# Seven block products in place of eight in two feed-forward chunks of each layer, with weight sums formed by accumulating transfers

## The chip, the core and the metric

The kernel runs on one core of a Trainium2 chip. A core has TensorE (PE, matrix products; its weight loads are shown apart as PEld), VectorE (DVE), ScalarE (ACT), GpSimd (POOL) and SyncE (SP). SP and POOL also start transfers, which all run on the core's 16 DMA engines. The metric is the device time of one execution in microseconds (us). Less is better.

## The reference, cut to what matters

Two layers over 256 positions of width 1024 in float32. Each layer has a mixing half and a feed-forward half; the change is in the second:

```
h2 = rms_norm(x, ln2_g[l])
x = x + (jax.nn.silu(h2 @ w_ff_gate[l]) * (h2 @ w_ff_up[l])) @ w_ff_down[l]
```

`w_ff_gate` and `w_ff_up` are 1024 x 2816, `w_ff_down` is 2816 x 1024.

## The kernel before, in words

**Precision.** Every float32 operand is split in two float32r halves, `h` (high) and `l` (low). A product is three TensorE products: high by high, high by low, low by high (`products`, L228 to L234). One of them has a 128x128 stationary operand (positions) and 512 moving columns (weights).

**Weights.** All weights stream from memory once, as units of 512 KB (128 partitions x 1024 floats), in the order in which `plan` lists them. `load` (L172 to L186) starts a unit's transfer on SP's queue into one of six staging buffers `st`. `making` (L192 to L204) splits a unit: ACT copies `st` into `wh` (L200), DVE subtracts to get `wl` (L201), and the next load is issued into the staging buffer that this frees. There are five pairs `wh`/`wl` (`RING`), so a unit can be made when TensorE is done with the unit five places ahead of it in the order.

**Feed-forward half.** The 2816 hidden columns are cut in five chunks of 512 and one of 256. A full chunk `c` (`gate_up`) is four gate units, then four up units, each against both row blocks of 128 positions (`project`): 2 matrices x 2 row blocks x 8 slices of 128 inputs x 3 = 96 products. Then SiLU (L864), the product with the up half (L853), four transposes for each row block and a split (`hidden`) make the next operand, and four down units (`down_units`, 12 products each) apply the part of the hidden columns that the chunk before made. So a full chunk is 12 units and 144 products.

**Order.** `Flow` runs side tasks (SiLU, `hidden`) a step at a time after each half unit (`atom_done`); a scheduler then sets each engine's list. Each engine works its list strictly in order, and so do SP's and POOL's queues of transfers.

**Names for the change.** With positions cut in two row blocks and the 1024 inputs in two halves, the operand is four blocks a11, a12, a21, a22 (`norm2.sets`), and the weights of a chunk are b11, b21 (gate, upper and lower half of the inputs) and b12, b22 (up). Each weight block is two units.

## Time and profile before

| what | value |
|---|---|
| runs | 762.56 us median of 3 (762.29 to 763.51) |
| profiled execution | 763.14 us, of which the span from first to last instruction is 761.4 us |
| granted TensorE clock | 0.998 |
| feed-forward chunks of 512, layer 1 | the second from 223.6 to 257.2 us, the third to 290.8, the fourth to 324.4, the fifth to 358.0 |
| the same in layer 2 | the third from 629.5 to 663.1 us, the fifth from 696.7 to 730.3 |

Lines that begin with a letter and a number (L201) name a line of the kernel above. In a timeline a row is start, duration, engine, line, operation, output and inputs, and in brackets the idle time before it and what ended that. A row of windows gives, for a stretch of time, its length, then each engine's busy time with its number of instructions, the granted clock, the share of time in which the 16 DMA engines were busy, and the rate. A row of groups gives the number of instructions, their busy time in us and the mean of one in ns, then idle time before them and what ended it. Products overlap in TensorE's pipeline, so the time of one product is read from the distance of starts, not from its own duration.

### The profile page before, as it was taken

To read this page: it belongs to the slowest core of one execution; us is meant where nothing else is said; L and a number is where in the kernel's file an instruction comes from. 1 tells how busy PE (TensorE), PEld (TensorE's weight loads), DVE (VectorE), ACT (ScalarE), POOL (GpSimd) and SP (SyncE) were. 2 spreads that over 40 slices of the span, in tenths; PEclk is the share of its full clock that TensorE was granted. 3 is DMA by queue.
4 is the path that set the end of the run, shared out by engine and by line. 5 is a ranking of instruction groups with operands and counts; after the bars stand their busy time and mean duration, and the time that the engine had idled before them with its cause. 6 is when DMAs were issued, how large, how long until landed. Compare 5 with 4: busy or idle time off the path is not lost.

```text
span 761.4 us, 9611 instructions
## 1 busy us (share of the span) xinstructions
PE 751.4 (99%) x3473; PEld 618.4 (81%) x3473; DVE 485.9 (64%) x705; ACT 407.5 (54%) x603; POOL 81.3 (11%) x115
## 2 busy tenths in 40 slices
PE   8998999999999999999999999999999999999998
PEld 6777888888888888888888788888888888888886
DVE  5688876677655454545577968776865554555543
ACT  6649665454654444444386966554556444444440
POOL 1442000310100000000011420121101000000000
PEclk9999999999999999999999999999999999999999
DMA  6995545676666566655655555475566666666621
GB/s 209 328 309 171 172 154 183 206 219 181 179 194 178 183 194 192 184 188 182 193 168 165 169 162 171 135 228 198 182 176 184 189 184 187 186 194 193 194 84 55
DMA packets 70315, 140.91 MB, mean 185 GB/s; under 512 B 5574, under 2 KB 11324, under 8 KB 70268
## 3 DMA queue, kind: packets, MB, share of 16 engines
q1 hardware_dynamic: 68844, 136.48, 58.0%
q0 software_dynamic: 1424, 3.82, 2.1%
q8 instruction: 27, 0.44, 0.2%
q14 instruction: 20, 0.16, 0.1%
HBM read 139.23 MB, written 1.84 MB: 185 GB/s over the span
## 4 chain that ended last, share of the span: by engine, by line
PE 90%; DVE 3%; ACT 2%; DMA 2%; POOL 1%; issue 1%; SPq 1%
PE acc L234 19%; PE acc L232 19%; PE acc L233 19%; PE tp L232 9%; PE tp L234 9%; PE tp L233 9%; PE tp L260 4%; DMA st<-in_w_in_dram 2%; PE tp L651 1%; DVE wl L201 1%; ACT wh L200 1%; PE tp L686 1%; POOL rr L284 1%; DVE xc L482 0%; POOL bnrv L553 0%
## 5 line engine op out<-in xcount | busy, mean ns | idle before, releaser
L201 DVE TENSOR_TENSOR wl<-st,wh 128x1024 fp32r<-128x1024 f32 (+1 forms) x253 | 311.9, 1234 | 228.5 <-ACT wh L200 228.3
L200 ACT ACTIVATE wh<-st 128x1024 fp32r<-128x1024 f32 (+1 forms) x253 | 267.1, 1057 | 264.6 <-PE acc L234 143.0
L232 PE MATMUL acc<-wh,ah 128*128 128x512 f32 x704 | 283.8, 403 | 0.0
L233 PE MATMUL acc<-wl,ah 128*128 128x512 f32 x704 | 275.2, 391 | 0.8 <-DVE cqz L392 0.8
L234 PE MATMUL acc<-wh,al 128*128 128x512 f32 x704 | 275.8, 392 | 0.0
L234 PEld LDWEIGHTS acc<-wh,al 128*128 128x128 f32 x704 | 132.4, 188 | 28.3
L233 PEld LDWEIGHTS acc<-wl,ah 128*128 128x128 f32 x704 | 132.8, 189 | 26.3 <-DVE cqz L392 1.1
L232 PEld LDWEIGHTS acc<-wh,ah 128*128 128x128 f32 x704 | 132.6, 188 | 26.0 <-issue 0.6
L232 PE MATMUL tp<-wh,ah 128*128 128x512 f32 x288 | 112.4, 390 | 0.0
L234 PE MATMUL tp<-wh,al 128*128 128x512 f32 x288 | 112.1, 389 | 0.0
L233 PE MATMUL tp<-wl,ah 128*128 128x512 f32 x288 | 112.0, 389 | 0.0
L234 PEld LDWEIGHTS tp<-wh,al 128*128 128x128 f32 x288 | 54.1, 188 | 11.3
L233 PEld LDWEIGHTS tp<-wl,ah 128*128 128x128 f32 x288 | 54.1, 188 | 11.1
L232 PEld LDWEIGHTS tp<-wh,ah 128*128 128x128 f32 x288 | 54.1, 188 | 11.1
L305 POOL TENSOR_TENSOR nss<-nsq 128x1 f32<-128x1 f32 x8 | 3.6, 449 | 262.1 <-ACT junk L301 262.1
L266 ACT ACTIVATE ah<-tp 128x512 fp32r<-128x512 f32 (+1 forms) x32 | 18.0, 562 | 11.8 <-PE tp L260 11.8
L777 POOL TENSOR_TENSOR merged<-merged,tg 128x512 f32<-128x512 f32 x12 | 19.2, 1623 | 39.4 <-DVE tg L774 39.4
L267 DVE TENSOR_TENSOR al<-tp,ah 128x512 fp32r<-128x512 f32 (+1 forms) x32 | 20.5, 652 | 0.0
L655 ACT ACTIVATE s<-s,nm 128x128 f32<-128x128 f32 (+1 forms) x32 | 14.3, 447 | 8.7 <-DVE nm L653 8.7
L765 DVE SCALAR_TENSOR_TENSOR tg<-acc,rstd,bg 128x512 f32<-128x512 f32 x24 | 17.1, 742 | 0.0
L812 POOL DMA_DIRECT2D bg<-in_b_gate_dram x12 | 7.0, 582 | 93.4 <-DVE tg L765 92.0
L766 ACT ACTIVATE tg<-tg 128x512 f32<-128x512 f32 x24 | 14.2, 621 | 4.3 <-DVE tg L765 4.3
(181 smaller groups left out, 492.0 us busy)
## 6 DMA issues: line engine op xcount, KB each, us to landing
st<-in_w_in_dram SPq DMA_DIRECT2D x87, 512.0 KB
st<-in_w_ff_down_dram SPq DMA_DIRECT2D x44, 512.0 KB
st<-in_w_ff_gate_dram SPq DMA_DIRECT2D x40, 512.0 KB
st<-in_w_ff_up_dram SPq DMA_DIRECT2D x40, 512.0 KB
st<-in_w_o_dram SPq DMA_DIRECT2D x16, 512.0 KB
st<-in_w_pc_dram SPq DMA_DIRECT2D x8, 512.0 KB
bg<-in_b_gate_dram POOLq DMA_DIRECT2D x12, 256.0 KB, 4.8
st<-in_w_pa_dram SPq DMA_DIRECT2D x4, 512.0 KB
```

What stands on the lines that cost most here:

```text
L200: state["wh"] = nc.scalar.activation(wh[:, k], st[:, k], AF.Copy).ins
L201: state["wl"] = nc.vector.tensor_tensor(wl[:, k], st[:, k], wh[:, k].bitcast(F32), ALU.subtract).ins
L232: nc.tensor.matmul(acc, ah[:, k, :], wh[:, kk, cols], start=first, stop=False)
L233: nc.tensor.matmul(acc, ah[:, k, :], wl[:, kk, cols], start=False, stop=False)
L234: state["pe"] = nc.tensor.matmul(acc, al[:, k, :], wh[:, kk, cols], start=False, stop=last).ins
L260: nc.tensor.transpose(tp[:, (at + j) * P:(at + j + 1) * P], src[:, j * P:(j + 1) * P], ident)
L266: nc.scalar.activation(h_, ps[:, :k * P], AF.Copy)
L267: nc.vector.tensor_tensor(l_, ps[:, :k * P], h_.bitcast(F32), ALU.subtract)
L655: nc.scalar.activation(st[:, c, :nk], st[:, c, :nk], AF.Exp, scale=-1.0, bias=nm[:, c:c + 1], accum_out=ss[:, c:c + 1])
L765: nc.vector.scalar_tensor_tensor(t, acc[r], rstd[r], bg, ALU.mult, ALU.add)
L766: nc.scalar.activation(t, t, AF.Tanh, scale=0.5)
L777: eng.tensor_tensor(m, m, g, ALU.add)
```

## The change

In the third and the fifth chunk of each layer (`c` = 2 and 4) the 2x2 block product of operand blocks and weight blocks is formed by seven block products in place of eight (a Strassen-Winograd scheme). A block product is one row block by one weight block: two units, 12 TensorE products. The seven right-hand sides are b11, b21, b11+b12, b11+b12+b22, b22, b12+b22 and b11+b12+b22+b21.

- Weight sums. b11 is loaded into a staging pair x (in the buffers of `merged`), b12 into a pair y (in the buffers of `qz`), both as plain transfers on SP. The other weights are added to them by POOL transfers with `accum_op=add`: b22 to y, and one after the other b12, b22 and b21 to x. Each sum on x can start only when ACT and DVE have split the version before it. b21 and b22 are also loaded as units of their own.
- Each version is split into `wh` and `wl`: 14 makings for the gate and up weights in place of 8. A unit of these feeds one row block, 6 products, in place of two row blocks, 12 products.
- Operand sums (`block_sums`). Eight POOL additions of 128x512 per layer rebuild and combine the operand blocks, and four ACT copies and four DVE subtractions split the results (s1 to s4).
- Results (`seven`). x and z are PSUM banks that go on collecting over several block products; ACT copies three part results out of them and DVE adds or subtracts three times. The four down units stand between the blocks.
- `load` keeps at most five ring units ahead (`AHEAD`) and starts a staging pair when it comes up in the order.
- The chunk after a seven uses other PSUM banks and ends the seven's last side task behind its own gate and up.

```diff
+AHEAD = 5
+SEVEN = (2, 4)
...
+        def seven(c):
+            def half(w, kh):
+                return [rows(w, 4 * kh + 2 * u, 2, c * NW, (c + 1) * NW) for u in range(2)]
+            b11, b21 = (half(a["w_ff_gate"][l], kh) for kh in range(2))
+            b12, b22 = (half(a["w_ff_up"][l], kh) for kh in range(2))
+            ks = iter(range(4 * c - 4, 4 * c))
+            x = [unit([(0, NW, b11[u])], "merged") for u in range(2)]
+            y = [unit([(0, NW, b12[u])], "qz") for u in range(2)]
+            cuts[-1][1].extend((y[u], b22[u]) for u in range(2))
+            cuts.extend((x[u], [(x[u], b12[u])]) for u in range(2))
+            for u in range(2):
+                cut([(0, NW, b21[u])])
+            down_cut(next(ks))
+            cuts.extend((x[u], [(x[u], b22[u])]) for u in range(2))
+            down_cut(next(ks))
+            down_cut(next(ks))
+            cuts.extend((x[u], [(x[u], b21[u])]) for u in range(2))
+            for u in range(2):
+                cut([(0, NW, b22[u])])
+            cuts.extend((y[u], []) for u in range(2))
+            down_cut(next(ks))
+            cuts.extend((x[u], []) for u in range(2))
...
+        while state["loads"] < len(loads):
+            i = state["loads"]
+            slot, parts = loads[i]
+            n = parts[-1][1]
+            if slot is None:
+                if state["out"] == AHEAD:
+                    return
+                tag = f"st{state['ring'] % STAGES}"
+                state["ring"] += 1
+                state["out"] += 1
             else:
+                tag = slot
+                if sum(loads[j][0] == slot for j in staged) == 2:
+                    return
+            state["loads"] += 1
+            if slot is None:
+                st = ring.tile([P, 1024 // n, n], F32, tag=tag, name="st")
+            else:
+                st = work.tile([P, 1024 // n, n], F32, tag=tag, bufs=2, name="st")
...
         i = len(made)
-        st = staged[i]
-        staged[i] = None
+        j, adds = cuts[i]
+        while j not in staged:
+            load()
+        st = staged[j]
         wh = ring.tile(list(st.shape), F32R, tag=f"wh{i % RING}", name="wh")
         wl = ring.tile(list(st.shape), F32R, tag=f"wl{i % RING}", name="wl")
         made.append((wh, wl))
...
             state["wh"] = nc.scalar.activation(wh[:, k], st[:, k], AF.Copy).ins
             state["wl"] = nc.vector.tensor_tensor(wl[:, k], st[:, k], wh[:, k].bitcast(F32), ALU.subtract).ins
             yield
-        if len(staged) < len(units):
-            load()
+        for m, src in adds:
+            nc.gpsimd.dma_start(staged[m], src, accum_op=ALU.add)
+        if last_cut[j] == i:
+            del staged[j]
+            state["out"] -= loads[j][0] is None
+        load()
...
+        s_ops = {}
+        def block_sums():
+            t = {}
+            for r in range(NR):
+                for n in range(2):
+                    ah, al = norm2.sets[r][n]
+                    t[r, n] = t2k("sum").rearrange("p (k n) -> p k n", n=P)
+                    nc.gpsimd.tensor_tensor(t[r, n], ah.bitcast(F32), al.bitcast(F32), ALU.add)
+                    yield 1
+            for name, at, o, p, q, op in (("s1", "vv", (1, 1), (1, 0), (1, 1), ALU.subtract),
+                                      ("s3", "o", (1, 0), (0, 0), (1, 0), ALU.subtract),
+                                      ("s2", "nat", (0, 0), (1, 1), (0, 0), ALU.subtract),
+                                      ("s4", "sq", (0, 1), (0, 1), (0, 0), ALU.add)):
+                nc.gpsimd.tensor_tensor(t[o], t[p], t[q], op)
+                yield 1
+                sh, sl = (work.tile([P, 4, P], F32R, tag=at, bufs=2, name=n) for n in ("sh", "sl"))
+                nc.scalar.activation(sh, t[o], AF.Copy)
+                nc.vector.tensor_tensor(sl, t[o], sh.bitcast(F32), ALU.subtract)
+                s_ops[name] = sh, sl
+                yield 1
+        def block(bank, lhs, first):
+            for u in range(2):
+                w = take()
+                for kk in range(2):
+                    k = 2 * u + kk
+                    products(bank, lhs, k, w, kk, slice(0, NW), first and k == 0, k == 3, skip_group_check=True)
+                release()
+                atom_done()
+        def half_hidden(c, r, t, sg):
+            nc.vector.scalar_tensor_tensor(sg, t, rstd2[r], sg, ALU.mult, ALU.mult)
+            yield 3
+            tp = tp_bank(3)
+            transpose(tp, sg, 4)
+            hsets[c, r] = split(tp, 4)
+            yield 1
+        def seven(c):
+            (a11, a12), (_, a22) = norm2.sets
+            ks = iter(range(4 * c - 4, 4 * c))
+            x, w = tp_bank(0), tp_bank(1)
+            def copy(bank):
+                t = t2k("part")
+                nc.scalar.activation(t, bank, AF.Copy)
+                return t
+            def gate0(t):
+                nc.vector.tensor_tensor(t, t, w, ALU.add)
+                nc.scalar.activation(t, t, AF.Silu, scale=rstd2[0])
+                yield 1
+            block(x, a11, True)
+            g0 = copy(x)
+            block(w, a12, True)
+            flow.start(gate0(g0))
+            down_units([next(ks)])
+            z = tp_bank(2)
+            block(z, s_ops["s1"], True)
+            u1 = copy(z)
+            down_units([next(ks)])
+            down_units([next(ks)])
+            block(x, s_ops["s2"], False)
+            u0 = copy(x)
+            block(z, s_ops["s4"], False)
+            nc.vector.tensor_tensor(u0, z, u0, ALU.subtract)
+            flow.add(half_hidden(c, 0, u0, g0), 1)
+            block(x, s_ops["s3"], False)
+            nc.vector.tensor_tensor(u1, u1, x, ALU.subtract)
+            down_units([next(ks)])
+            block(x, a22, False)
+            g1 = t2k("sg")
+            nc.scalar.activation(g1, x, AF.Silu, scale=rstd2[1])
+            return flow.add(half_hidden(c, 1, u1, g1), 1)
...
-                ga = accs() if c == 0 else [tp_bank(0), tp_bank(1)]
+                first, second = ((1, 2), (0, 3)) if c - 1 in SEVEN else ((0, 1), (2, 3))
+                ga = accs() if c == 0 else [tp_bank(b) for b in first]
                 project(norm2.sets, 4, ga)
                 ts = flow.add(silu(ga, NW, sg))
-                ua = accs() if c == 0 else [tp_bank(2), tp_bank(3)]
+                ua = accs() if c == 0 else [tp_bank(b) for b in second]
                 project(norm2.sets, 4, ua)
                 flow.finish(ts)
-                return flow.add(hidden(c, sg, ua, NW, (0, 1) if c else (2, 3)))
-            ga = [tp_bank(0), tp_bank(1)]
+                return flow.add(hidden(c, sg, ua, NW, first if c else (2, 3)))
...
+        flow.add(block_sums(), 18)
+        th = None
         for c in range(nfull + 1):
-            th = gate_up(c)
+            if c in SEVEN:
+                th = seven(c)
+                continue
+            if th is not None and c - 1 in SEVEN:
+                before = th
+                th = gate_up(c)
+                flow.finish(before)
+            else:
+                th = gate_up(c)
```

The three places that the change is about, as the engines' lists have them. In them `st_2311` and `st_2313` are the two buffers of x, `st_2315` and `st_2317` those of y in the third chunk of the first layer, and `st_2826` to `st_2832` the same for the fifth.

First POOL's list in the feed-forward half of the first layer. Before, from the second row block's statistics of this layer to the first ones of the next:

```order
L305 TENSOR_TENSOR nss_2085<-nsq_1782 128x1
L283 TENSOR_SCALAR rstd_1784<-nss_2085 128x1
L284 TENSOR_TENSOR rstd_1784<-rstd_1784,mhalf_81 128x1
L305 TENSOR_TENSOR nss_3521<-nsq_1991 128x1
L283 TENSOR_SCALAR rstd_1993<-nss_3521 128x1
```

And with the change, from the last operand sum to the sums for the fifth chunk:

```order
L959 TENSOR_TENSOR sum_2236<-sum_2236,sum_2213 128x512
L276 DMA st_2311<-in_w_ff_up_dram 128x2x512
L276 DMA st_2313<-in_w_ff_up_dram 128x2x512
L276 DMA st_2311<-in_w_ff_up_dram 128x2x512
L276 DMA st_2313<-in_w_ff_up_dram 128x2x512
L276 DMA st_2311<-in_w_ff_gate_dram 128x2x512
L276 DMA st_2313<-in_w_ff_gate_dram 128x2x512
L276 DMA st_2830<-in_w_ff_up_dram 128x2x512
L276 DMA st_2832<-in_w_ff_up_dram 128x2x512
```

Where POOL had nothing, it now has six sums into x in three pairs, and then the two into y of the fifth chunk. (The two into y of the third chunk stand much earlier, among POOL's loads of the gates' bias.)

Second ACT's list in the third chunk of the first layer. Before, in the stretch of the up units, one making of a fresh unit after the other:

```order
L864 ACTIVATE sg_2547<-tp_2459,rstd_1783 128x512
L200 ACTIVATE wh_2541<-st_2471 128x1024
L864 ACTIVATE sg_2549<-tp_2460,rstd_1784 128x512
L200 ACTIVATE wh_2563<-st_2489 128x1024
L200 ACTIVATE wh_2581<-st_2507 128x1024
L200 ACTIVATE wh_2599<-st_2525 128x1024
```

With the change, from the second version of x (b11+b12) to the third (b11+b12+b22):

```order
L272 ACTIVATE wh_2517<-st_2311 128x1024
L993 ACTIVATE part_2522<-tp_2497 128x512
L272 ACTIVATE wh_2530<-st_2313 128x1024
L272 ACTIVATE wh_2541<-st_2393 128x1024
L272 ACTIVATE wh_2555<-st_2416 128x1024
L998 ACTIVATE part_2522<-part_2522,rstd_1783 128x512
L272 ACTIVATE wh_2574<-st_2311 128x1024
L272 ACTIVATE wh_2585<-st_2313 128x1024
L993 ACTIVATE part_2590<-tp_2567 128x512
```

The makings of x's versions now stand among those of fresh units, and part results are copied from PSUM between them.

Third DVE's list at the end of the third chunk. Before, around the product with the up half:

```order
L201 TENSOR_TENSOR wl_2600<-st_2525,wh_2599 128x1024
L853 SCALAR_TENSOR_TENSOR sg_2547<-tp_2533,rstd_1783,sg_2547 128x512
L853 SCALAR_TENSOR_TENSOR sg_2549<-tp_2534,rstd_1784,sg_2549 128x512
L201 TENSOR_TENSOR wl_2618<-st_2545,wh_2617 128x1024
L201 TENSOR_TENSOR wl_2647<-st_2567,wh_2646 128x1024
```

With the change, from the last version of x to the second unit of the fourth chunk (`tp_2567` is PSUM bank z, `tp_2497` is bank x, `part_2648` and `part_2590` are the up halves of the two row blocks):

```order
L273 TENSOR_TENSOR wl_2669<-st_2311,wh_2668 128x1024
L1014 TENSOR_TENSOR part_2648<-tp_2567,part_2648 128x512
L273 TENSOR_TENSOR wl_2680<-st_2313,wh_2679 128x1024
L977 SCALAR_TENSOR_TENSOR part_2522<-part_2648,rstd_1783,part_2522 128x512
L273 TENSOR_TENSOR wl_2691<-st_2545,wh_2690 128x1024
L1017 TENSOR_TENSOR part_2590<-part_2590,tp_2497 128x512
L273 TENSOR_TENSOR wl_2704<-st_2559,wh_2703 128x1024
```

The product with the up half (L977) and the subtraction that frees bank x for the last block (L1017) now stand behind the making of x's last version.

More of the change, by code (lines that the diff above doesn't have):

```diff
@@ L139, in trunk, with unit, cut, down_cut @@
     gates_order = [(0, 0), (1, 0), (2, 0), (0, 1), "merge0", (1, 1), (2, 1), "merge1"]
+    loads, cuts = [], []
+    def unit(parts, slot=None):
+        loads.append((slot, parts))
+        return len(loads) - 1
     def plan(l):
+        def cut(parts):
+            cuts.append((unit(parts), []))
         def cols(w, c, n=4):
-            return [[(0, NW, rows(w, 2 * u, 2, c * NW, (c + 1) * NW))] for u in range(n)]
+            for u in range(n):
+                cut([(0, NW, rows(w, 2 * u, 2, c * NW, (c + 1) * NW))])
+        def down_cut(k):
+            cut([(0, D, wd[k * P:(k + 1) * P, :].unsqueeze(1))])
+        def seven(c):
[20 more added lines that the diff above has]
+            cuts.extend((x[u], []) for u in range(2))
@@ L154, in plan @@
         for n in range(2):
-            res += cols(a["w_o"][l], n)
+            cols(a["w_o"][l], n)
         for c in range(nfull + 1):
+            if c in SEVEN:
+                seven(c)
+                continue
             if c < nfull:
-                res += cols(a["w_ff_gate"][l], c) + cols(a["w_ff_up"][l], c)
+                cols(a["w_ff_gate"][l], c)
+                cols(a["w_ff_up"][l], c)
             else:
                 lo, hi = c * NW, FFN
-                res += [[(0, rest, rows(a["w_ff_gate"][l], 2 * u, 2, lo, hi)),
-                         (rest, 2 * rest, rows(a["w_ff_up"][l], 2 * u, 2, lo, hi))] for u in range(4)]
+                for u in range(4):
+                    cut([(0, rest, rows(a["w_ff_gate"][l], 2 * u, 2, lo, hi)),
+                         (rest, 2 * rest, rows(a["w_ff_up"][l], 2 * u, 2, lo, hi))])
@@ L163, in plan @@
             if c:
[L164 to L170 removed]
+                for k in range(4 * c - 4, 4 * c):
+                    down_cut(k)
+        for k in range(4 * nfull, nk_down):
+            down_cut(k)
@@ L171, in trunk @@
+    for l in range(DEPTH):
+        plan(l)
+    last_cut = {i: n for n, (i, _) in enumerate(cuts)}
+    staged, made = {}, []
+    state = {"taken": 0, "atom": 0, "loads": 0, "ring": 0, "out": 0}
     freed = []
     def load(between=None):
-        i = len(staged)
-        parts = units[i]
-        n = parts[-1][1]
-        st = ring.tile([P, 1024 // n, n], F32, tag=f"st{i % STAGES}", name="st")
-        for lo, hi, src in parts:
-            if i == 0:
-                for k in range(1024 // n):
-                    nc.sync.dma_start(st[:, k:k + 1, lo:hi], src[:, k:k + 1, :])
-                    if k == 0:
-                        between()
-            else:
-                state["load"] = nc.sync.dma_start(st[:, :, lo:hi], src).ins
@@ L186, in load @@
-        staged.append(st)
+        while state["loads"] < len(loads):
[8 more added lines that the diff above has]
+                state["out"] += 1
+            else:
+                tag = slot
[6 more added lines that the diff above has]
+                st = work.tile([P, 1024 // n, n], F32, tag=tag, bufs=2, name="st")
+            for lo, hi, src in parts:
+                if i == 0:
+                    for k in range(1024 // n):
+                        nc.sync.dma_start(st[:, k:k + 1, lo:hi], src[:, k:k + 1, :])
+                        if k == 0:
+                            between()
+                else:
+                    state["load"] = nc.sync.dma_start(st[:, :, lo:hi], src).ins
+            staged[i] = st
+            if slot is None:
+                return
@@ L227, in atom_done, with products @@
         flow.tick()
-    def products(acc, lhs, k, w, kk, cols, first, last):
+    def products(acc, lhs, k, w, kk, cols, first, last, **kw):
         (ah, al), (wh, wl) = lhs, w
-        nc.tensor.matmul(acc, ah[:, k, :], wh[:, kk, cols], start=first, stop=False)
-        nc.tensor.matmul(acc, ah[:, k, :], wl[:, kk, cols], start=False, stop=False)
-        state["pe"] = nc.tensor.matmul(acc, al[:, k, :], wh[:, kk, cols], start=False, stop=last).ins
+        nc.tensor.matmul(acc, ah[:, k, :], wh[:, kk, cols], start=first, stop=False, **kw)
+        nc.tensor.matmul(acc, ah[:, k, :], wl[:, kk, cols], start=False, stop=False, **kw)
+        state["pe"] = nc.tensor.matmul(acc, al[:, k, :], wh[:, kk, cols], start=False, stop=last, **kw).ins
     def project(sets, nunits, acc):
```

24 lines of the change are left out of this document (12 added, 12 removed).

## The prediction

> **What bounds the kernel now.** First the page's sums and the chain of work that ended last, then the stretches of the feed-forward half, then single rows of TensorE, ACT and DVE there.
>
> ```profile
> PE 751.4 (99%) x3473; PEld 618.4 (81%) x3473; DVE 485.9 (64%) x705; ACT 407.5 (54%) x603; POOL 81.3 (11%) x115
> PE 90%; DVE 3%; ACT 2%; DMA 2%; POOL 1%; issue 1%; SPq 1%
> ```
>
> TensorE carries 90% of the chain, so a product that is left out is worth its time there, unless something else comes to end late. The stretches: one of the start, at full DMA load, and the second, third and fourth feed-forward chunk.
>
> ```profile
> core 0: us, PE busy (x) PEld busy (x) DVE busy (x) ACT busy (x) POOL busy (x), PEclk, DMA share, GB/s
> 20.00:40.00 20.00, 19.23 (x87) 14.58 (x86) 15.01 (x41) 13.64 (x24) 8.61 (x19) 1.00 1.02 331
> ...
> 223.60:257.20 33.60, 33.60 (x157) 27.84 (x156) 18.79 (x19) 15.47 (x18) 0.00 (x0) 1.00 0.61 187
> 257.20:290.80 33.60, 33.60 (x153) 27.81 (x153) 17.29 (x16) 15.08 (x16) 0.00 (x0) 1.00 0.63 188
> 290.80:324.40 33.60, 33.60 (x153) 27.81 (x152) 17.29 (x16) 15.08 (x16) 0.00 (x0) 1.00 0.63 188
> ```
>
> In a chunk TensorE is never idle, DVE is busy for half of it, POOL not at all, and the DMA engines have a third to spare. The third chunk's beginning, in rows of three engines:
>
> ```profile
> 254.72 1.06 ACT L200 ACTIVATE wh<-st 128x1024 fp32r<-128x1024 f32 x1 [1.66 <-PE acc L234]
> ...
> 255.81 1.23 DVE L201 TENSOR_TENSOR wl<-st,wh 128x1024 fp32r<-128x1024 f32 x1 [1.50 <-ACT wh L200]
> 255.88 0.39 PE L232 MATMUL acc<-wh,ah 128*128 128x512 f32 x1
> ...
> 257.44 1.06 ACT L200 ACTIVATE wh<-st 128x1024 fp32r<-128x1024 f32 x1 [1.66 <-PE acc L234]
> ...
> 261.32 0.39 PE L232 MATMUL tp<-wh,ah 128*128 128x512 f32 x1
> ```
>
> Between the two L232 rows 24 products start: 5.44/24 = 0.2267 us each. A unit of 12 takes 2.72 us, which is also the distance of ACT's makings, and each making waits 1.66 us for TensorE to free a `wh` buffer. So the makings run as early as the five buffers let them.
>
> **What goes.** Seven blocks in place of eight are 84 products in place of 96, in four chunks: 48 products fewer, 48 x 0.2267 = 10.9 us. The transposes stay: 33.60 - 144 x 0.2267 = 0.96 us for eight of them. A seven lasts 132 x 0.2267 + 0.96 = 30.9 us if TensorE never waits.
>
> **What comes, beside other work.** The rest of the prices:
>
> ```profile
> L201 DVE TENSOR_TENSOR wl<-st,wh 128x1024 fp32r<-128x1024 f32 (+1 forms) x253 | 311.9, 1234 | 228.5 <-ACT wh L200 228.3
> L200 ACT ACTIVATE wh<-st 128x1024 fp32r<-128x1024 f32 (+1 forms) x253 | 267.1, 1057 | 264.6 <-PE acc L234 143.0
> L853 DVE SCALAR_TENSOR_TENSOR sg<-tp,rstd,sg 128x512 f32<-128x512 f32 x16 | 11.2, 742 | 0.0
> L267 DVE TENSOR_TENSOR al<-tp,ah 128x512 fp32r<-128x512 f32 x28 | 19.0, 686 | 0.0
> L864 ACT ACTIVATE sg<-tp,rstd 128x512 f32<-128x512 f32 x16 | 10.9, 679 | 2.4 <-PE tp L234 2.4
> L777 POOL TENSOR_TENSOR merged<-merged,tg 128x512 f32<-128x512 f32 x12 | 19.2, 1623 | 39.4 <-DVE tg L774 39.4
> ```
>
> Six makings more in each seven: 7.4 us of DVE, 6.3 of ACT. DVE then has 18 x 1.23 for makings, 3 x 0.69 for results (priced as L267), 2 x 0.74 and 2 x 0.69, together 27.1 of 30.9 us; ACT 18 x 1.06 + 5 x 0.68 + 2 x 0.69 = 23.9. Both still fit. The operand sums are eight POOL operations of 1.6 us and four pairs of ACT and DVE, some 13 us in the first two chunks of a layer, where POOL is idle and DVE has 15 us free per chunk. I cost them at nothing; without that cover it would be up to 13 us a layer, since the first s operand is needed 8 us into the third chunk.
>
> Transfers: a seven needs 20 units where a chunk needed 12. The four plain loads of x and y start a chunk or more before, and y's sums too. At 0.63 busy for 188 GB/s the engines would move 298 GB/s if full, 1.76 us per unit. Third to fifth chunk together need 46 units from 257 us on, 81 us of 95. Cost nothing by themselves, if a sum's transfer takes no longer than a plain one.
>
> The y loads and sums of the third chunk have been moved far ahead, past others on SP and POOL:
>
> ```profile
> 86.71 0.37 SPq L185 DMA_DIRECT2D st<-in_w_in_dram  x1
> 90.03 0.37 SPq L185 DMA_DIRECT2D st<-in_w_in_dram  x1
> ...
> 101.51 0.37 SPq L185 DMA_DIRECT2D st<-in_w_pa_dram  x1
> 107.47 0.37 SPq L185 DMA_DIRECT2D st<-in_w_pb_dram  x1
> ...
> 89.16 0.61 PE L651 MATMUL tp<-kT,qz 128*128 128x128 f32 x4
> ...
> 104.96 1.03 PE L651 MATMUL tp<-kT,qz 128*128 128x256 f32 x4
> ...
> 92.56 0.61 POOL L812 DMA_DIRECT2D bg<-in_b_gate_dram  x1 [18.32 <-DVE tg L765]
> 103.56 0.19 POOL L283 TENSOR_SCALAR ro<-sso 128x4 f32<-128x4 f32 x1 [10.40 <-DVE sso L697]
> ```
>
> The load of y's first buffer stands on SP between the two loads of input weights at 86.71 and 90.03, and waits for the last product that reads the first `qz`, over at 89.8. So it fits into the gap, and its sum follows on POOL behind the bias load at 92.56, where POOL was idle for 10.4 us. The second stands between the loads at 101.51 and 107.47, and its `qz` is read until 106.0. If SP held the load at 107.47 for a microsecond, the units ahead would cover it: nothing.
>
> **What comes on the path.** x passes through four versions. Each sum waits for the split of the one before, and the next split waits for the sum to land, on ACT and DVE, which work in order. So the path is sum, split, sum, split, and then what stands behind it on DVE. The trace has no accumulating transfer; the nearest rows are POOL's plain loads:
>
> ```profile
> bg<-in_b_gate_dram POOLq DMA_DIRECT2D x12, 256.0 KB, 4.8
> ...
> DMA to landing us min/median/max: 3.6/4.8/6.7
> ```
>
> 256 KB from issue to landing 4.8 us, 3.6 to 6.7. For 512 KB 0.9 us more: L = 5.7 (4.5 to 7.6). If each byte of a sum costs the engines two, since the destination is read as well: 7.4 (6.2 to 9.3).
>
> Now the chunk from its first product (times worked out from the rows above). x's second buffer, which is the later one: the first block ends at 2.7; ACT then copies a part (0.68) and makes `wh` (1.06), DVE `wl` (1.23): the second version is split at 5.8 and its sum goes out. It lands at 5.8 + L2. Split 2.3 us: the next sum goes out at 8.1 + L2 and lands at 8.1 + L2 + L3. Then ACT 1.06, and on DVE in this order the making, L977, the making of the next chunk's first unit and L1017, 1.23 + 0.74 + 1.23 + 0.69: the last block may start at 13.1 + L2 + L3. TensorE gets there at 27.2 + four transposes 0.5 = 27.7. So **two sums have 14.6 us**; what they take more, TensorE stands still, in each of four chunks, and at 14.6 + 10.9/4 = 17.3 us, 8.7 for one, the gain is gone. Without any lateness the same list ends at 27.7 as well, since L1014 waits for z's last block at 21.8 and 5.8 us of DVE work follow: no slack, for which I take 0.3 us a chunk.
>
> A pair of sums is sent 2 us apart, and ring loads pass at the same time. At the plain price the pair doesn't overlap, and half a ring unit more makes L 6.6: 13.2, hidden. I take a transfer between the plain and the doubled price, nearer to the plain row because that is the one of the same queue: L = 7.5, sum 15.0, 0.4 late. With the 0.3 that is 0.7 x 4 = 2.8 us.
>
> **Sum**: 10.9 - 2.8 = 8.1 us less. The profiled execution took 763.14 us (span 761.4), 0.6 over the median, so 755.0 by its own time; against the median 762.56 it is **754.5 us**. With no stall it is 751.7.
>
> **Rivals.**
>
> 1. *Slower: a sum costs the engines double.* Then L2 = 7.4 + 1.5 (the second of a pair waits for the first, 3.5 us long and 2 us ahead) + 0.9 (ring load) = 9.8, and L3 = 7.4 + 0.9 = 8.3: 18.1, a stall of 3.5 + 0.3, in four chunks 15.2 us: 766.9 us. With the longest landing of bias loads (1.9 more each) the stall is 7.6: 782. For it: a sum has to read what it adds to. Also for it: with 14 doubled sums the third to fifth chunk need 60 x 1.76 = 106 us of the engines in 95. Against it: the stretch from 20 to 40 us moved 331 GB/s, by which it would be 95, and 4.8 us for half the size is mostly not transfer, so the part that doubles is small. It decides from 8.7 us per sum on.
> The Trainium skill speaks for this one: "Collectives: The Full Stack", "The bandwidth ceiling: the fold count and why AG ≠ RS ≠ AR", says that a reduction in the DMA engines runs at half the rate of a copy, as it reads two sources for each write. No run here shows it yet; by it the time is this rival's 767, by the plain row 752 to 753.
> 2. *DVE becomes the bound.* 27.1 of 30.9 us leaves 3.8, and in the trace DVE's making grows when POOL reads at the same time:
>
> ```profile
> 135.92 1.23 DVE L201 TENSOR_TENSOR wl<-st,wh 128x1024 fp32r<-128x1024 f32 x1 [0.30 <-ACT wh L200]
> ...
> 138.63 1.56 DVE L201 TENSOR_TENSOR wl<-st,wh 128x1024 fp32r<-128x1024 f32 x1 [0.30 <-ACT wh L200]
> ...
> 137.83 3.53 POOL L777 TENSOR_TENSOR merged<-merged,tg 128x512 f32<-128x512 f32 x2 [3.95 <-DVE tg L774]
> ```
>
> If the last eight makings of a seven took 1.56 too and all of it reached TensorE, it is 2.6 us a chunk: 751.7 + 10.6 = 762.3, the same as before. POOL does no arithmetic there, so I think little of it.
> 3. *The change saves no products.* The engine lists show 48 fewer on TensorE, so this can't be.
>
> **Chances.** Sums hidden or nearly (L up to 8.2, 751 to 758.5): 0.56. Sums at 8.2 to 8.5 or some DVE lateness (to 761): 0.07. Break-even or DVE bound (761 to 764): 0.08. Doubled or longer (over 764): 0.29, of which half over 770. So faster 0.63, same 0.08, slower 0.29, where "same" is within 0.2% (1.5 us), about what a measurement here can tell. The range that leaves out no more than 2 in 10 is 751 to 770; the likeliest case by itself is 751 to 758.5.
>
> **What will show it.** TensorE 48 products fewer, 24 makings more (277), POOL's queue with 16.8 MB more. Right if a seven, begun at about 257, lasts some 31 to 32 us, sums land in 6 to 8 us, and TensorE's only wait is the one at the last block, on DVE. Wrong if sums take over 8.7: then ACT's making waits for DMA twice per seven, DVE behind it, and TensorE at the third version and at the last block. Wrong in another way if ACT or TensorE waits for POOL's operand sums in the first two chunks, or if the stretch around 90 to 110 us has grown.

## The result and the profile after

The changed kernel takes **753.36 us** (median of 4 runs, 752.27 to 754.39) where the kernel before takes 762.68 (4 runs, 762.29 to 763.51) on the same chip: a ratio of 0.9879, 95% interval 0.9864 to 0.9893, 9.3 us less. A second set of runs (after_again below) gave 753.46 and 0.9879 again. The profiled execution of after took 753.26 us, its span 751.5, at a granted clock of 1.0. So 754.5 was 1.1 us too high.

From the page of after: busy time by engine, the chain that ended last, the makings, and the queue of POOL (packets, MB, share of the 16 engines' span).

```profile
PE 741.1 (99%) x3425; PEld 608.3 (81%) x3425; DVE 530.8 (71%) x749; ACT 438.8 (58%) x647; POOL 148.0 (20%) x163
q0 software_dynamic: 10128, 20.60, 15.4%
PE 82%; DVE 6%; DMA 5%; issue 2%; POOL 2%; ACT 2%; SPq 1%; ACTq 0%; DVEq 0%; POOLq 0%
L273 DVE TENSOR_TENSOR wl<-st,wh 128x1024 fp32r<-128x1024 f32 (+1 forms) x277 | 342.3, 1244 | 173.2 <-ACT wh L272 171.8
```

48 products fewer and 24 makings more, as forecast. TensorE's share of the chain has fallen from 90% to 82%: the chain now leaves TensorE for sums, makings and DVE here and there, though TensorE is still 99% busy. That is what a near tie looks like.

Where the time came from is read between marks on TensorE: the first product of a chunk's down units. From the first chunk's mark to the third's lies the third chunk's gate and up, from there to the fifth's mark the fifth's. The windows between the marks, both layers, of before and then of after:

```profile
245.41:312.58 67.17, 67.17 (x305) 55.62 (x304) 34.58 (x33) 30.16 (x32) 0.00 (x0) 1.00 0.63 188
312.58:368.88 56.30, 56.30 (x258) 46.61 (x256) 29.70 (x29) 25.12 (x27) 0.00 (x0) 1.00 0.59 187
617.29:684.47 67.18, 67.18 (x306) 55.63 (x305) 34.59 (x33) 30.16 (x32) 0.00 (x0) 1.00 0.63 188
684.47:740.76 56.29, 56.29 (x258) 46.61 (x256) 29.68 (x29) 25.12 (x27) 0.00 (x0) 1.00 0.50 160
```

```profile
243.94:309.35 65.41, 64.93 (x293) 53.41 (x292) 42.77 (x42) 36.88 (x41) 9.58 (x8) 1.00 0.93 257
309.35:363.21 53.86, 53.86 (x245) 44.36 (x244) 37.86 (x38) 31.97 (x36) 7.15 (x6) 1.00 0.82 214
611.64:676.92 65.28, 64.94 (x294) 53.41 (x292) 42.78 (x42) 36.88 (x41) 9.64 (x8) 1.00 0.93 258
676.92:730.81 53.89, 53.89 (x246) 44.37 (x245) 37.98 (x38) 32.16 (x36) 7.15 (x6) 1.00 0.73 185
```

The four stretches are 1.76, 2.44, 1.90 and 2.40 us shorter: **8.50 us**. Twelve products are 2.72, so 10.88 were to be had and 2.4 were lost. The rest of the 9.9 us between the two spans, 1.5, lies ahead of the first mark (245.41 against 243.94); it moves from run to run, since over the kernels below the first mark lies between 243.7 and 246.4. The stretch between the layers (368.88 to 617.29 before, 363.21 to 611.64 now) is 248.4 us in both, so nothing is won or lost outside the sevens.

The path that the prediction worked out, in timelines of after: first the seven that starts at 255.77, then the fifth chunk's, which starts at 321.20. The POOL rows are the issues of x's sums, the ACT rows the makings that wait for them to land.

```profile
261.79 1.19 POOL L276 DMA_DIRECT2D st<-in_w_ff_up_dram  x1 [0.66 <-DVE wl L273]
272.99 1.19 POOL L276 DMA_DIRECT2D st<-in_w_ff_gate_dram  x1 [3.40 <-DVE wl L273]
...
270.38 1.06 ACT L272 ACTIVATE wh<-st 128x1024 fp32r<-128x1024 f32 x1 [3.52 <-DMA st<-in_w_ff_up_dram]
279.43 2.96 ACT L272 ACTIVATE wh<-st 128x1024 fp32r<-128x1024 f32 x3 [1.34 <-DMA st<-in_w_ff_gate_dram]
...
280.53 1.23 DVE L273 TENSOR_TENSOR wl<-st,wh 128x1024 fp32r<-128x1024 f32 x1
281.67 0.75 DVE L977 SCALAR_TENSOR_TENSOR part<-part,rstd 128x512 f32<-128x512 f32 x1
282.33 1.22 DVE L273 TENSOR_TENSOR wl<-st,wh 128x1024 fp32r<-128x1024 f32 x1
283.47 0.68 DVE L1017 TENSOR_TENSOR part<-part,tp 128x512 f32<-128x512 f32 x1
...
283.22 0.60 PE L336 MATMUL tp<-ident,part 128*128 128x128 f32 x4
284.30 0.47 PE L308 MATMUL tp<-wh,ah 128*128 128x512 f32 x1 [0.48 <-DVE part L1017]
...
327.23 1.19 POOL L276 DMA_DIRECT2D st<-in_w_ff_up_dram  x1 [0.66 <-DVE wl L273]
337.89 1.19 POOL L276 DMA_DIRECT2D st<-in_w_ff_gate_dram  x1 [1.96 <-DVE wl L273]
...
335.27 1.06 ACT L272 ACTIVATE wh<-st 128x1024 fp32r<-128x1024 f32 x1 [2.09 <-DMA st<-in_w_ff_up_dram]
344.15 3.04 ACT L272 ACTIVATE wh<-st 128x1024 fp32r<-128x1024 f32 x3 [1.13 <-DMA st<-in_w_ff_gate_dram]
```

In the third chunk L2 is 270.38 - 261.79 = 8.6 us and L3 279.43 - 272.99 = 6.4, together 15.0. In the fifth they are 8.0 and 6.3, 14.3, and TensorE has no wait there. The list of waits gives 0.48 us for L1017 in the third chunk, but that is not all of it: the last block starts 284.30 - 283.22 = 1.08 us after the first transpose, where in the fifth, without a wait, it is 0.36 (348.66 and 349.02). So the block is 0.7 late, not the 0.4 that 15.0 against the forecast 14.6 would be. What two sums really have is 14.3 us: the first goes out 6.0 us after the seven's start (261.79 - 255.77) in place of 5.8, the split between the two takes 2.6 (270.38 to 272.99) in place of 2.3, 4.87 follow the second landing, and TensorE is there at 27.8 (349.02 - 321.20).

### The profile page after: what moved, and what is told of

The parts are those of the page before. It is cut to its first block, busy times and chain, and to the rows that moved or that the text cites. A ratio compares the mean times of both kernels' runs of the same rounds, so it can differ in the third digit from the quotient of the medians.

```text
span 751.5 us, 9745 instructions
## 1 busy us (share of the span) xinstructions
PE 741.1 (99%) x3425; PEld 608.3 (81%) x3425; DVE 530.8 (71%) x749; ACT 438.8 (58%) x647; POOL 148.0 (20%) x163
## 4 chain that ended last, share of the span: by engine, by line
PE 82%; DVE 6%; DMA 5%; issue 2%; POOL 2%; ACT 2%; SPq 1%; ACTq 0%; DVEq 0%; POOLq 0%
PE acc L310 18%; PE acc L308 18%; PE acc L309 18%; PE tp L308 8%; PE tp L310 8%; PE tp L309 8%; DMA st<-in_w_in_dram 3%; PE tp L336 3%; DVE wl L273 2%; ACT wh L272 2%; PE tp L727 1%; DMA st<-in_w_ff_up_dram 1%; POOL rr L360 1%; DMA st<-in_w_ff_gate_dram 1%; PE tp L762 1%
## 5 line engine op out<-in xcount | busy, mean ns | idle before, releaser
L273 DVE TENSOR_TENSOR wl<-st,wh 128x1024 fp32r<-128x1024 f32 (+1 forms) x277 | 342.3, 1244 | 173.2 <-ACT wh L272 171.8
L272 ACT ACTIVATE wh<-st 128x1024 fp32r<-128x1024 f32 (+1 forms) x277 | 289.5, 1055 | 218.3 <-PE acc L310 119.2
L308 PE MATMUL tp<-wh,ah 128*128 128x512 f32 x208 | 82.1, 395 | 0.8 <-DVE part L1017 0.8
L310 PE MATMUL tp<-wh,al 128*128 128x512 f32 x208 | 81.1, 390 | 0.0
L309 PE MATMUL tp<-wl,ah 128*128 128x512 f32 x208 | 81.0, 389 | 0.0
L276 POOL DMA_DIRECT2D st<-in_w_ff_up_dram x24 | 28.9, 1222 | 176.5 <-DVE wl L273 163.8
L310 PEld LDWEIGHTS tp<-wh,al 128*128 128x128 f32 x208 | 39.0, 188 | 8.3
L310 PE MATMUL tp<-wh,sl 128*128 128x512 f32 x64 | 25.2, 394 | 0.0
L309 PE MATMUL tp<-wl,sh 128*128 128x512 f32 x64 | 25.2, 394 | 0.0
L308 PE MATMUL tp<-wh,sh 128*128 128x512 f32 x64 | 25.2, 393 | 0.0
L342 ACT ACTIVATE ah<-tp 128x512 fp32r<-128x512 f32 (+1 forms) x32 | 17.9, 560 | 9.0 <-PE tp L336 9.0
```

Source lines behind the costliest of these rows:

```text
L272: state["wh"] = nc.scalar.activation(wh[:, k], st[:, k], AF.Copy).ins
L273: state["wl"] = nc.vector.tensor_tensor(wl[:, k], st[:, k], wh[:, k].bitcast(F32), ALU.subtract).ins
L276: nc.gpsimd.dma_start(staged[m], src, accum_op=ALU.add)
L308: nc.tensor.matmul(acc, ah[:, k, :], wh[:, kk, cols], start=first, stop=False, **kw)
L309: nc.tensor.matmul(acc, ah[:, k, :], wl[:, kk, cols], start=False, stop=False, **kw)
L310: state["pe"] = nc.tensor.matmul(acc, al[:, k, :], wh[:, kk, cols], start=False, stop=last, **kw).ins
```

## The experiments

All but after_again, which is the changed kernel once more, are edits of the changed kernel. Each ratio is against runs of the kernel before on the same chip, and ratios are compared rather than medians; for the small terms the distance of the marks is used, which does not contain the start. Of the chunks below: 67.17 and 56.30 us before, 65.41 (65.28 in layer 2) and 53.86 (53.89) after.

| kernel | time us | ratio to before (95%) | third chunk, layers 1 and 2 | fifth chunk |
|---|---|---|---|---|
| e1_plain | 753.06 | 0.985 to 0.989 | 64.75, 64.75 | 53.89, 53.89 |
| e2_twice | 795.27 | 1.0402 to 1.0437 | 78.17, 76.72 | 64.25, 63.25 |
| e3_third | 759.86 | 0.9946 to 0.9977 | 65.22, 65.13 | 56.31, 56.31 |
| e4_fifth | 757.27 | 0.9911 to 0.9942 | 67.17, 67.17 | 53.87, 53.87 |
| e5_nosums | 754.73 | 0.9869 to 0.9914 | 64.79, 65.08 | 53.98, 53.89 |
| e6_extra | 764.11 | 1.0003 to 1.0023 | 67.46, 67.47 | 56.61, 56.60 |
| after_again | 753.46 | 0.9864 to 0.9894 | 65.05, 64.93 | 53.88, 53.89 |
| e7_hold | 753.92 | 0.9872 to 0.9902 | 65.04, 64.75 | 53.88, 53.88 |
| e8_early | 753.03 | 0.9860 to 0.9893 | 64.91, 64.87 | 53.89, 53.89 |
| e9_both | 753.43 | 0.9866 to 0.9903 | 64.75, 64.74 | 53.88, 53.88 |
| e10_place | 755.14 | 0.9882 to 0.9916 | 65.14, 64.91 | 54.41, 53.90 |
| e11_shift | 755.38 | 0.9885 to 0.9934 | 66.54, 65.05 | 53.89, 53.89 |

The theory: the products are worth their price, and what is lost is lost at the last block, because x's two sums land late. The rivals: sums so dear that they eat the gain, and a loss that has nothing to do with the sums.

### One seven a layer

```diff
-SEVEN = (2, 4)
+SEVEN = (2,)     # e3_third
+SEVEN = (4,)     # e4_fifth
```

> Seven blocks in the third chunk of each layer alone, the fifth as before. From the two traces (distance of TensorE's down units): a third chunk with its successor saves 1.8 to 1.9 us, a fifth 2.4. So 3.7 us less than before: 759. Rival (the two have a common cost, or help each other): not between 758 and 760.

> Seven blocks in the fifth chunk of each layer alone. By the same distances 4.85 us less than before: 757.8. If the third chunk's greater loss comes from what stands around it (y's sums far ahead, the first x sums on an idle POOL) and not from the seven as such, the fifth alone should lose as little as in the change.

The fifth alone brings 5.8 us and the third alone 3.2, together 8.9. By the marks it is 2.43 and 2.42 us in the fifth chunks and 1.95 and 2.05 in the third. So the two don't disturb each other, and in these profiles the third is the one that loses more.

### What a sum costs over a plain transfer

```diff
-            nc.gpsimd.dma_start(staged[m], src, accum_op=ALU.add)
+            nc.gpsimd.dma_start(staged[m], src)
```

> All as in the change, but POOL's 32 transfers overwrite their destination where they added to it (this leaves out the weight sums). Theory (a sum moves its bytes at about half the rate of a copy, but landing is mostly fixed, so the sums are nearly hidden): landing falls from 6.3 us by 0.5 to 1.5 us, that of the second of a pair by up to 3, TensorE's wait on L1017 (0.8 us in all) goes, and the time falls by 0.5 to 1.5 us: 752 to 753. Rival (the adding itself costs what was lost of the 10.9 us): down by 2.4 us, to 751.0. Rival (adding is free): same landing, 753.4.

The row of POOL's sums from the up weights, first of after, then of e1 (duration of the issue in ns, min/median/max), with the landing times of all 32; then POOL's queue in e1:

```profile
L276 POOL DMA_DIRECT2D st<-in_w_ff_up_dram x24: 1182/1194/1640, 92.8 to 694.8; - x24
...
DMA to landing us min/median/max: 5.6/6.3/13.6
```

```profile
L276 POOL DMA_DIRECT2D st<-in_w_ff_up_dram x24: 722/722/809, 94.1 to 693.7; - x24
...
DMA to landing us min/median/max: 3.9/4.8/8.7
```

```profile
q0 software_dynamic: 6032, 20.60, 9.6%
```

Adding lengthens the landing by 1.5 us at the median, 6.3 in place of 4.8. In e1 no seven is late: the four stretches are 64.75 and 53.89. The end of DVE's list and TensorE's last block, in the first of them:

```profile
282.55 0.68 DVE L1017 TENSOR_TENSOR part<-part,tp 128x512 f32<-128x512 f32 x1
...
283.29 0.60 PE L336 MATMUL tp<-ident,part 128*128 128x128 f32 x4
283.64 0.48 PE L308 MATMUL tp<-wh,ah 128*128 128x512 f32 x1
```

So without lateness L1017 is over at 283.23, 0.4 us before the block starts: the list has that much slack. The price of a sum at the engines is larger, in proportion, than that of its landing. The queue had 2.1% of the engines' time before the change:

```profile
q0 software_dynamic: 1424, 3.82, 2.1%
```

So the 16.8 MB cost 7.5% of the span plain and 13.3% added, 1.8 times as much, and 1.9 times the packets (272 a sum in place of 144). For one transfer that is, estimated as the share of the span over 32, 3.1 us of all 16 engines in place of 1.8, 1.4 us more, which is about what the landing grew by. The Trainium skill's rule that rival 1 rested on ("Collectives: The Full Stack", "The bandwidth ceiling: the fold count and why AG ≠ RS ≠ AR": a reduction reads two sources, so it runs at half the rate of a copy, told there of ring collectives) is nearly borne out for the engines' time. It does not carry over to the whole landing, of which 1.8 of 4.8 us are engines' time by the estimate above: that grew 1.3 times. Between the marks of the third chunk the engines were 0.93 busy in after and 0.77 in e1.

What all lateness of the sums costs in after is read off the marks: 65.41 - 64.75 and 65.28 - 64.75, 0.66 and 0.53 us in the third chunks, nothing in the fifth: 1.2 us in all. The median differs from after's by less than the runs differ among themselves.

### One sum more on the path

```diff
-            cuts.extend((x[u], [(x[u], b21[u])]) for u in range(2))
+            cuts.extend((x[u], [(x[u], b21[u])] * (1 + u)) for u in range(2))
```

> The last sum into x's second buffer (b21) is sent twice, so one landing more, some 6.3 us, stands on the path from the third version to the last (this adds b21 twice to that half). Theory (two sums have 14.6 us in a seven, used up now; then DVE's list L273, L977, L273, L1017 follows): each seven gets longer by 6 to 6.3 us, all of it in TensorE's wait for L1017 and the transposes ahead of it: 753.4 + 25 = 778. Rival (sums lie off the path by some microseconds, what was lost of the 10.9 us is elsewhere): under 760.

It cost 42 us, far more than either theory said. The direction and the place are the theory's; the size is not. The first seven of e2 in the timeline, and one stretch in windows:

```profile
281.44 1.18 POOL L276 DMA_DIRECT2D st<-in_w_ff_gate_dram  x1 [5.43 <-DMA st<-in_w_ff_gate_dram]
285.44 2.53 POOL L276 DMA_DIRECT2D st<-in_w_ff_up_dram  x2 [2.81 <-DMA st<-in_w_ff_up_dram]
...
291.26 3.90 ACT L272 ACTIVATE wh<-st 128x1024 fp32r<-128x1024 f32 x4 [11.34 <-DMA st<-in_w_ff_gate_dram]
...
294.29 1.11 PE L336 MATMUL tp<-ident,part 128*128 128x128 f32 x4 [9.91 <-DVE part L977]
296.11 0.77 PE L308 MATMUL tp<-wh,ah 128*128 128x512 f32 x1 [0.71 <-ACT ah L342]
296.68 0.63 PE L309 MATMUL tp<-wl,ah 128*128 128x512 f32 x1
297.11 0.63 PE L310 MATMUL tp<-wh,al 128*128 128x512 f32 x1
...
300.38 0.40 PE L309 MATMUL tp<-wl,ah 128*128 128x512 f32 x1
```

```profile
285.00:300.00 15.00, 5.00 (x13) 3.85 (x14) 6.49 (x7) 5.44 (x6) 2.38 (x2) 0.55 1.05 264
```

Two things were left out of the expectation. First, the added sum took 291.26 - 281.44 = 9.8 us; the DMA engines were full meanwhile (1.05 in this stretch), and y's sums for the fifth chunk went out at 285.44, which is the likely reason. From its landing to the last block is 4.85 us, as in after (4.87). Second, TensorE stood still for 9.9 us, and behind that products follow each other at 0.43 us in place of 0.23 until 300.1, at a granted clock of 0.55 for the stretch. The waits of TensorE for L977 add to 30.4 us, those for the split behind it (L342) to 2.8; the four stretches are 44.0 us longer than in after, so some 11 us are the slow products and transposes behind four stalls. The Trainium skill has this ("TensorE: Matmul & The Clock Gate", "🔬 Part 1: The HAM clock gate (the "warmup" mystery)": a few microseconds without work halve the clock, and it takes some 4 us of work to return); the trace agrees, with about 4 us at half rate. The lesson for the prediction: its rivals priced a stall at its own length, and a stall of this size cost a third more.

### The work off the path

```diff
-                    t[r, n] = t2k("sum").rearrange("p (k n) -> p k n", n=P)
-                    nc.gpsimd.tensor_tensor(t[r, n], ah.bitcast(F32), al.bitcast(F32), ALU.add)
+                    t[r, n] = ah.bitcast(F32)
...
-                nc.gpsimd.tensor_tensor(t[o], t[p], t[q], op)
```

> The eight POOL additions of operand blocks per layer are left out; ACT and DVE split other blocks instead (this leaves out the operand sums). Theory (they lie beside other work, POOL and DVE have room in the first two chunks): same time within 0.5 us of the change, 753 to 753.9, although DVE's makings get shorter there. Rival (POOL's reads slow DVE and ACT waits for POOL, 3.1 us by the list of waits, and some reaches TensorE): down by 1.5 to 3 us, 750.5 to 752.

Without POOL's operand sums it took 754.73 (runs from 752.30 to 756.33), no faster than after, and the fifth chunk is the same within 0.12 us. Its third chunks lie between e1's and after's. So these sums cost nothing that the runs can show, as forecast. The windows from 202 us to the first mark say why, before and then after:

```profile
202.00:245.41 43.41, 43.41 (x200) 35.91 (x199) 23.84 (x29) 23.48 (x32) 3.30 (x6) 1.00 0.62 189
```

```profile
202.00:243.94 41.94, 41.94 (x192) 34.69 (x191) 29.36 (x32) 24.38 (x34) 16.11 (x12) 1.00 0.61 189
```

POOL goes from 3.3 to 16.1 us and DVE from 23.8 to 29.4, while TensorE is busy for all of both stretches.

The other way round, the 48 products are put back, into a bank that nobody reads, and everything else of the change stays:

```diff
-        def block(bank, lhs, first):
+        def block(bank, lhs, first, spare=None):
...
+                    if spare is not None:
+                        products(spare, lhs, k, w, kk, slice(0, NW), k == 0, k == 3)
...
-            block(w, a12, True)
+            block(w, a12, True, tp_bank(3))
```

> The b21 block is multiplied twice, the second time into a PSUM bank that nobody reads: the 12 products that a seven saves are done again, all else as in the change. Theory (the gain is the products' own time, and TensorE's wait at the last block is lateness of sums, which 2.7 us more in mid-chunk cover): 753.4 + 10.9 less the 0.8 to 2 us of waits: 762.3 to 763.5, with no wait on L1017. Rival (part of the gain came from the new order of loads or makings): clearly under 761.

```profile
245.86:313.32 67.46, 67.46 (x305) 55.66 (x304) 43.33 (x42) 37.57 (x41) 9.58 (x8) 1.00 0.90 249
```

With the products of before, the kernel is 0.13% slower than before (1.0003 to 1.0023), 0.6 us above the top of what was expected. So the makings, sums and transfers together are hidden to about a microsecond (0.13% of 762.5), and the gain is the products. This gives the sums 2.7 us more time per seven as well, so it doesn't show that the path is hidden in after. But it shows something new: 0.29 and 0.31 us more per stretch than before for the same number of products, with TensorE never idle. Four times that, 1.2 us, is the whole excess of e6.

### The last microseconds at the last block

Three edits try to win back what L1017 costs: no making of the next chunk's unit at the end of the s3 block, so that it can't stand ahead of L1017 (e7); one of the down units moved behind the b11+b12 block, so that the later blocks come later (e8); and both (e9).

```diff
-            block(x, s_ops["s3"], False)
+            block(x, s_ops["s3"], False, hold=True)   # e7: at its last unit only count the atom and tick the side tasks
```

```diff
             flow.start(gate0(g0))
-            down_units([next(ks)])
             z = tp_bank(2)
...
             down_units([next(ks)])
+            down_units([next(ks)])
             down_units([next(ks)])
```

> The change once more, to be compared with the three next ones on the same chip: 753.4 us (0.988 of before), a stall of about 0.5 us at the last block of the third chunks (L1017), none in the fifth.

> One making held back: in a seven no unit is made at the end of the block before the last, so that DVE's list has L1017 ahead of the next chunk's first making. Theory (the DVE list behind the last sum decides when the last block starts): 1.2 us earlier, so TensorE's waits on it (0.8 us in all) go: 752.3 to 752.8. Rival (the third version's lateness has to be made up anyway, or the held making is late in its turn): 753.4 or more.

> A seven's first down unit stands behind the block of b11+b12 instead of ahead of it, so that x's second version is made some 2 us earlier and the two sums have some 16.6 us instead of 14.6. Theory: lateness of sums goes in the third chunks, but the same DVE list, bound by z's last block, still ends where TensorE gets to: 752.2 to 753. Rival (lateness is not what is lost): 753.4.

> Both edits. Theory: nothing is late any more and the whole 10.9 us is had: 751.2 to 752, no wait of TensorE in a seven. Rival (another loss, as in the chunk after a seven): 752.3 or more.

The first result is the unedited one. In after_again the list of waits has no L1017 at all, where 0.5 us was expected:

```profile
243.66:308.71 65.05, 64.98 (x294) 53.41 (x292) 42.75 (x42) 36.79 (x41) 9.58 (x8) 1.00 0.92 259
```

```profile
282.94 0.60 PE L336 MATMUL tp<-ident,part 128*128 128x128 f32 x4
283.61 0.47 PE L308 MATMUL tp<-wh,ah 128*128 128x512 f32 x1
```

The block starts 0.67 us after the first transpose, so it is 0.3 late and not 0.7. How late it is differs between executions of one kernel, and it follows the landings. The table has the sixteen sevens of four profiles in which the engines work the same lists there (e10 and e11, of the next section, only move buffers). Each entry is L2 + L3, and then by how much the stretch is longer than 64.75 (third chunk) or 53.89 (fifth), its length where nothing is late, in us:

| kernel | third, layer 1 | third, layer 2 | fifth, layer 1 | fifth, layer 2 |
|---|---|---|---|---|
| after | 15.0: 0.66 | 14.9: 0.53 | 14.3: 0 | 13.9: 0 |
| after_again | 14.6: 0.30 | 14.5: 0.18 | 14.3: 0 | 13.9: 0 |
| e10_place | 14.7: 0.39 | 14.4: 0.16 | 14.9: 0.52 | 13.9: 0 |
| e11_shift | 16.1: 1.79 | 14.6: 0.30 | 14.0: 0 | 13.7: 0 |

Up to 14.3 us for the two sums nothing is lost; beyond it each microsecond of landing costs a microsecond, within 0.1. The fifth chunk obeys the same rule, as e10 shows; it is late less often because its sums land sooner. Why the landings of one kernel differ is open.

Of the edits, e9 is late in none of its four sevens, e8 by 0.16 and 0.12 in the third chunks, e7 by 0.29 in one of them. That one shows e7 at work: its two sums took 15.8 us, 1.5 over the 14.3, and it lost 1.2 less than that, the length of the making that was taken off the list. None of the three is measurably faster than after_again beside them. The first stretch of e9:

```profile
244.32:309.07 64.75, 64.75 (x294) 53.38 (x292) 42.82 (x42) 37.12 (x41) 9.58 (x8) 1.00 0.92 260
```

TensorE is busy throughout, and still a seven saves 2.42, not 2.72. That is e9's rival, another loss: 0.30 us in every seven, which no waiting explains. What e9 wins in its third chunks by the marks, 1.2 us against after and 0.5 against after_again, is less than what runs of one kernel differ by (e9's own: 752.44 to 755.29).

### Where 0.30 us goes in a seven without waits

First products of blocks in the first seven of after; between two of these rows stand 12 products with operand sums (s1; s2) or 24 (s4 and s3):

```profile
263.94 0.39 PE L308 MATMUL tp<-wh,sh 128*128 128x512 f32 x1
...
266.73 0.39 PE L308 MATMUL acc<-wh,ah 128*128 128x512 f32 x1
...
272.17 0.39 PE L308 MATMUL tp<-wh,sh 128*128 128x512 f32 x1
...
274.90 0.39 PE L308 MATMUL tp<-wh,sh 128*128 128x512 f32 x1
...
280.50 0.39 PE L308 MATMUL acc<-wh,ah 128*128 128x512 f32 x1
```

s1 takes 2.79 us, 0.2325 a product; s2 2.73, 0.2275; s4 and s3 5.60, 0.2333. A block with ordinary operands takes 2.72. So three of the four blocks are slower, by 0.23 us of the 0.30; where the rest lies is not shown. By the layout of the kernel's buffers (no trace shows an address) the pairs `sh`, `sl` of these three start at multiples of 64 bytes in a partition; that of s2, all other operands and the weights start 32 bytes behind one. Two kernels move them: e10 only what lies behind the convolution's tile, with it the three pairs; e11 everything.

```diff
-        xaT = work.tile([P, 2, S + CONV - 1], F32, tag="xaT", name="xaT")
+        xaT = work.tile([P, 2, S + CONV + 3], F32, tag="xaT", name="xaT")   # e10_place
```

```diff
+    pad = const.tile([P, 8], F32, name="pad")   # e11_shift, ahead of all other tiles
+    nc.vector.memset(pad, 0.0)
```

> The convolution's input tile is made 16 bytes a partition and column block wider, so that everything behind it in the on-chip memory starts 32 bytes later; nothing computed changes. In the profiles the products with the operand sums of s1, s4 and s3 follow each other at 0.2333 us, those with s2 at 0.2267 like all others. The pairs of s1, s3 and s4 start at multiples of 64 bytes, the pair of s2, the other operands and the weights 32 bytes behind one. Theory, the start address: all four at 32 behind, all 48 products at 0.2267, 36 x 0.0067 = 0.24 us less in each seven (a fifth chunk of 53.65 us between its marks instead of 53.89), 1.0 us less in all: 752.5. Rival, the operands' contents or their place among the buffers: 0.2333 stays in the same three blocks, 53.89 and 753.4.

> A tile of 32 bytes a partition ahead of all others moves every buffer by 32 bytes: weights, ordinary operands and the pair of s2 then start at multiples of 64, the pairs of s1, s3 and s4 do not. Theory, the start address of the stationary operand: the s2 block and every product with an ordinary operand go to 0.2333 us, the blocks of s1, s3 and s4 to 0.2267; of some 3,400 products nine tenths are of 512 columns, 3,000 x 0.0067 = 20 us more, about 773. Rival one, only the address against that of the weights matters: the relations are as they were, 753.4, with 0.2333 in the same three blocks. Rival two, the address of the weights alone, or of either operand: 0.2333 in all blocks, about 774. Rival three, contents or buffer: as rival one.

The same blocks in e10:

```profile
266.42 0.40 PE L308 MATMUL tp<-wh,sh 128*128 128x512 f32 x1
...
269.22 0.39 PE L308 MATMUL acc<-wh,ah 128*128 128x512 f32 x1
...
274.69 0.39 PE L308 MATMUL tp<-wh,sh 128*128 128x512 f32 x1
...
283.00 0.39 PE L308 MATMUL acc<-wh,ah 128*128 128x512 f32 x1
```

2.80 for s1 and 8.31 for the other three together, which in after is 8.33: nothing has changed. In e11 the s1 block takes 2.80 as well, though its pair now starts 32 bytes behind a multiple of 64, and a block with ordinary operands, now on multiples of 64, takes 2.73. The theory of the start address falls, by both. The two took 755.14 us (0.9882 to 0.9916 of before) and 755.38 (0.9885 to 0.9934): not faster than after, and the shifts gained nothing. e5, where the operands hold other values, shows the same distances (2.80 for s1, 8.33 for the other three together), so the values are not the cause either. What is left is that the three pairs lie in other buffers, by the layout farther up in the on-chip memory than s2's and the ordinary operands. That s operands in lower buffers would run at 0.2267 was not tried; the cause stays open.

## Why the prediction came out right

- **The products.** 48 x 0.2267 = 10.9 us was the right price: e6 puts them back and is at 764.1.
- **The path.** The last block of x as the only place of a wait in the sevens, L1017 as what it waits for, and 5.0 us from the last landing to the block's start (4.87 measured) held. The budget for two sums is 14.3 us, not 14.6: the terms ahead of the first sum and between the two were 0.2 and 0.3 too small, TensorE came 0.1 later than 27.7 (the prediction's own terms for its 5.8 add to 5.7). Two sums at 7.5 each, 15.0 together, are 15.0 in the third chunk of after, as 8.6 and 6.4, and 13.7 to 16.1 over the sixteen sevens.
- **The price of a sum was right by two misses that nearly cancel.** A plain 512 KB transfer lands in 4.8 us, not 5.7, and adding costs 1.5 us of landing, nearly the whole 1.7 of the doubled price. So "nearer to the plain row" is not what the runs show; that it gave the right sum is luck.
- **The loss of 2.8 us was made up otherwise.** It measured 2.4 in after: lateness 0.66 and 0.53 us in the third chunks and none in the fifth, 1.2 in place of 4 x 0.4; and 0.30 in each seven from slower products, which I had not seen, 1.2 in place of 4 x 0.3. In after_again it is 1.7. The step that failed is "no slack, for which I take 0.3 us a chunk". The prediction counted 5.8 us of DVE work behind L1014, but in the list that it goes by one of these makings stands ahead of L1014, so 4.6 follow. In e1, where no sum is late, the list ends 0.4 us before the block starts, and without lateness nothing is lost. In the third chunk of after the 0.3 only made up for the budget that was 0.3 too large. That the slower products cost the same 0.30 is chance.
- **Operand sums, transfers, the y loads moved ahead.** Nothing, as said: e5, the window from 202 us, and a first mark that is not later than before. The DMA engines' reserve was used up nearly whole, though (0.93 busy in the third chunk), which e2 shows by its price.
- **The rivals.** Doubled sums: nearly true of the engines and of what adding costs, but from a plain landing 0.9 us shorter than assumed. A sum landed in 6.3 us and not 7.4, two in the chunk took 15.0 and not 18.1, so the time didn't follow. DVE as the bound: the mean making grew from 1.234 to 1.244 us, not to 1.56.
- **The rest.** 1.5 of the 9.9 us between the profiled spans lie in the start, where the kernels differ from run to run; against the 8.5 of the sevens the forecast of 8.1 was 0.4 short, and 1.1 short of the 9.2 that the same marks give in after_again.

## What to carry to other kernels

When a product is traded for transfers and vector work, write down the one chain that has to be through before the last product, with its budget, and compare it with two or three of its own landings: here 15.0 against a measured 14.3 made the stretch 0.66 us longer, and 14.3 cost nothing. Price a possible miss by what happens behind it, too: with the DMA engines at 0.93, one sum more of 512 KB cost not its 6.3 us but 9.8, and the stall then slowed the products behind it. For tenths of a microsecond use the distance of marks inside one span; runs of one kernel here differ by 0.7 to 4.4 us and would have shown none of it. Take it from more than one profile: the same stretch of the same kernel was 65.41 us in one and 65.05 in the other, and the wait that the first one lists is not in the second one's list.

## What was unexpected of the hardware

- A transfer that adds made 1.9 times the packets of a plain one and took 1.8 times the engines' time (13.3% against 7.5% of the span for 32), 1.19 us of POOL for its issue in place of 0.72, but landed only 1.5 us later (512 KB: 6.3 against 4.8 us).
- Behind a stall of 9.9 us TensorE's products started 0.43 us apart in place of 0.23, until 5.8 us after its first instruction (294.29 to 300.09).
- The same product of 128x512 started every 0.2267 us with operands in most buffers and every 0.2333 with the operand sums s1, s3 and s4, at a granted clock of 1.0. Neither their values (e5) nor a shift of their start by 32 bytes (e10, e11) changed it.
